# Moving the loads of a seven-product kernel's last step: rows into T, late rows into two other buffers, a recombination put first

## The chip, the cores and the metric

The kernel runs on one core of a Trainium2 chip. The core has TensorE (PE; its weight loads are listed as PEld), VectorE (DVE), ScalarE (ACT), GpSimd (POOL) and SyncE (SP). SP's work here is to issue DMAs. GpSimd and ScalarE issue some too. The metric is the time of one execution on the device in microseconds. Three executions of the kernel before gave 893.77, 895.12 and 897.36 us, so the median is 895.12. The profiled execution took 893.32 us.

## The reference: what is computed

One layer on a sequence of 512 tokens (a grid of 8 by 64) with 2048 channels, all in float32:

```python
h = RMSNorm_pre(x)
q, k, v, z = split(h @ na_w_in, 4)         # each 512 x 2048, 16 heads of 128
o = neighbourhood_attention(q, k, v, rpb)  # window of 8 x 16 tokens, bias rpb, softmax
y = (o * silu(z)) @ na_w_out               # 512 x 2048
x = x + RMSNorm_post(y)
```

The input projection is 512 x 2048 by 2048 x 8192, the output projection 512 x 2048 by 2048 x 2048.

## The kernel before, in words

**Steps.** Both projections are cut into steps. Steps 0 to 7 make q, k, v and z of two heads each. Steps 8 and 9 make the two halves of the output projection. Steps 0 and 8 are plain: two column blocks (n=0 and 1) times sixteen slices of the contraction. The other steps multiply 2x2 blocks with seven products in place of eight (Strassen's scheme in Winograd's form). Each of these has seven passes of eight slices. A pass accumulates into a chain X, Y or Z of two PSUM banks (u7Z is chain Z of step 7), and after it `combine` adds the chains into the results. In the last step (LAST, step 9) the passes run in the order `LATE = (6, 0, 1, 3, 4, 5, 2)`.

**Rows.** The work is numbered by m, from 0 to N-1 = 511. A row m is one 128x512 tile of weights that takes part in the products of slice m. The plain step 8 is m=424 to 455, the last step m=456 to 511: P6 is 456 to 463, P0 464 to 471, P1 472 to 479, P3 480 to 487, P4 488 to 495, P5 496 to 503. Pass P2, 504 to 511, is prepared early as "late rows", between the rows of other passes, because nothing follows it that would hide its preparation. `prep(m)` makes a row ready: for some passes VectorE first adds a freshly loaded tile to the running sum T[k] (`t0` to `t7`); then ScalarE writes the high part `hi` (fp32r) and VectorE the low part `lo`, the source minus the high part. TensorE multiplies hi, hi and lo. hi and lo live in rings of three buffers. Rows are prepared AHEAD = 2 ahead of use. Late rows have their parts written into the tiles `a{k}_1` and `a{k}_3` of the activations (A), whose old contents are no longer used.

**Loads.** `load_raw` loads fresh tiles into a ring of four buffers ("raw"). Each load waits until VectorE has let go of the tile four before it, in the order in which VectorE releases them. `load_t` loads straight into T[k]. One sum of the last step (T1 in the change's name) is prepared during the plain step: eight tiles `zw0` to `zw7` are loaded into two buffers (`load_z`), VectorE adds `raw512` to `raw519` to them (`sum_prep`), and the eight sums are stored to DRAM (`wsum`, `keep_z`) and fetched back into T later. The residual x is loaded by `load_res` into tiles `xres` (for token blocks t=1, 2, 3) and into T[0..3] (t=0). The gated attention outputs go to DRAM (`graw`) and are fetched back on GpSimd's queue (`fetch_g`, tile gr12 among them); all the other loads go out on SP's queue.

**Attention beside it.** `HEAD` lists the operations of each head with a delay in units of m. At the end of head 15, the transposed probabilities (pt15_0, pt15_1) are split into high and low parts, TensorE multiplies them by v into o15, and `gated` writes zm15 from o15. o15 lies in the ring of PSUM banks that the accumulators j=2, 3 of the plain step's second column block use as well.

**What sets the order.** Calls through `sync`, `dve` and `act` are kept in program order on their engine. Everything else is placed by a scheduler that starts from the program order of the loop at the end (`prep`, then the products, then whatever `beside` lists for m). Each engine then runs its list strictly in order, so an instruction that waits holds up all behind it.

**The end.** `finish` weighs one block of the result: ScalarE squares it and sums, VectorE multiplies by the post norm's gain. For the last block (i=3) VectorE works out the mean square (`msy`), GpSimd raises it to the power -0.5, and `final` scales, adds the residual and sends the rows out.

Of the kernel before, what the change touches and what calls it, by code (L numbers as in the profile page):

```python
# [28 lines left out]
WARM = 8  # L29
# [39 lines left out]
def na_block(ctx: ExitStack, tc: tile.TileContext, xT, x, gpre, gpost, w, rpb, out):  # L69
# [61 lines left out]
    def load_z(k):  # L131
        Z[k] = cp.tile([P, L], F32, tag="zw", name=f"zw{k}", bufs=2)
        nc.sync.dma_start(Z[k], w[LAST, B12, k])

    def keep_z(k):
        nc.sync.dma_start(wsum[k], Z.pop(k))
# [87 lines left out]
    def is_raw(m):  # L224
        step, p, _ = where(m)
        return step in PLAIN or p not in ((0, 1, 6) if step == LAST else (0, 6))

    def late_prep(m):

        i, rest = divmod(m - (N - 4 * KH + 1), 3)  # L230
        return [N - KH + i] if 0 <= i < KH and not rest else []

    def sum_prep(m):

        m -= base(NSTEP)
        at_m = {6 + 2 * k: [k] for k in range(KH)}
        for k in range(KH):
            at_m.setdefault(22 + 2 * k if k < KH - 2 else 15 + 2 * k, []).append(KH + k)
        return [N + j for j in at_m.get(m, ())]
# [4 lines left out]
    seq = [m for m in preps if m >= N or is_raw(m)]  # L244
# [5 lines left out]
    def load_raw(m):  # L250
        raws[m] = wp.tile([P, L], F32, tag="raw", name=f"raw{m}", bufs=NRAW)
        if m >= N:
            i, k = divmod(m - N, KH)
            nc.sync.dma_start(raws[m], w[LAST, (B11, B22)[i], k])
            return
        step, p, k = where(m)
        if step in PLAIN:
            src = w[step, (B11, B12, B21, B22)[p + 2 * (k // KH)], k % KH]
        else:
            src = w[step, (None, B12, B21, B22, B21, B22, B22)[p], k]  # L260
        (sync if m < 3 else nc.sync).dma_start(raws[m], src)
# [3 lines left out]
    def prep(m):  # L265
# [22 lines left out]
        nc.vector.tensor_tensor(lo, src, hi.bitcast(F32), ALU.subtract)  # L288
        if plain:
            if step == 0 and p == 1 and k >= KH:  # L290
                load_t(1, B11, k - KH)
        elif p == 4 and step < LAST:
            load_t(step, B12, k)
        elif p == 5 and step < LAST:
            nc.vector.tensor_tensor(T[k], T[k], src, ALU.add)  # L295
        elif p == 6 and (step + 1 < NSTEP or step == LAST and k < KH - 2):
            load_t(min(step + 1, LAST), B11, k)
        elif p == 0 and step == LAST:
            nc.sync.dma_start(T[k], wsum[k])
# [12 lines left out]
    def mm_plain(m):  # L312
# [14 lines left out]
        if k == KT - 1:  # L327
            ops.sort(key=lambda op: op[2])
        for l, r, j, i in ops:
# [56 lines left out]
    def combine(step, p):  # L386
# [29 lines left out]
        else:  # L416
            for s in range(2):
                nc.vector.tensor_tensor(c["21"][:, s, :], u[s], c["21"][:, s, :], ALU.subtract)
                nc.vector.tensor_tensor(c["22"][:, s, :], c["22"][:, s, :], u[s], ALU.subtract)  # L419
# [289 lines left out]
    def finish(n, t, src, dst=None):  # L709
# [7 lines left out]
        def weigh():  # L717
            nc.scalar.activation(rest, src, AF.Square, accum_out=part[:, t, i : i + 1])
            nc.vector.tensor_tensor(y, src, gb[n], ALU.mult)  # L719
# [9 lines left out]
        if i == 3:  # L729
            nc.vector.tensor_scalar(msy[:, col], part[:, t, 3:4], 1.0 / D, ms3[:, col], ALU.mult, ALU.add)  # L730
            nc.gpsimd.tensor_tensor(rcy[:, col], msy[:, col], mhalf[:, 0:1], ALU.pow)

# [18 lines left out]
    for k in range(KH):  # L751
        at(base(NSTEP) + 1 + 2 * k, load_z, k)
# [6 lines left out]
    for q in range(4):  # L759
        at(base(LAST) + 4 + 3 * q, load_res, 1, q)  # L760
        at(base(LAST) + 4 * KH + 3 + 2 * q, load_res, 0, q)
    for i in range(KH):
        at(base(LAST) + 2 * KH + 5 * i // 2, load_res, 2 + i // 4, i % 4)
# [12 lines left out]
    for m in range(-AHEAD, N):  # L776
        if m + AHEAD < N - KH:
# [7 lines left out]
        (mm_plain if where(m)[0] in PLAIN else mm_seven)(m)  # L785
# [57 lines left out]
```

## Time and profile before

| | |
|---|---|
| median of three executions | 895.12 us (893.77 to 897.36) |
| profiled execution | 893.32 us, of which 891.5 us from the first to the last instruction (span) |
| granted TensorE clock | 0.998 of full speed |
| TensorE busy | 876.9 us, 98% of the span |
| VectorE, ScalarE, GpSimd busy | 734.3, 559.4 and 20.9 us |
| DMA | 174.95 MB, 196 GB/s on average |

The busy line says how long each engine worked. The lists of waits say for which group of instructions an engine stood idle and how long in total, how many times, and the longest. In a timeline each row has its start in microseconds, its length, the engine, the line, the operation and its tiles (numbers left out), and in brackets how long the engine was idle before it and what released it. `x4` means four instructions in a row. A table of windows has, for each stretch, its length, the busy time and the instructions of each engine, the granted clock, the busy share of the DMA engines and GB/s.

### The profile page before, as it was taken

How to read it: one execution, taken by the hardware profiler on the slowest of the kernel's cores; microseconds unless marked ns; L12 is line 12 of the kernel's file. 1: busy time of each engine (PE TensorE's matmuls, PEld its weight loads, DVE VectorE, ACT ScalarE, POOL GpSimd, SP SyncE). 2: the span in 40 equal slices, each digit the busy share in tenths (PEclk: the TensorE clock that was granted, in tenths of full speed). 3: DMA queues.
4: the chain of work that ended last, by engine and by line, in shares of the span. 5: the costliest groups of instructions: out<-in, count | busy, mean ns of one | idle time of the engine just before them, and what ended most of it. 6: DMA issues, size and time to landing. Idle time of an engine off the chain costs nothing. (4 is left out here: it accounts for less than half of the span.)

```text
span 891.5 us, 13143 instructions
## 1 busy us (share of the span) xinstructions
PE 876.9 (98%) x4176; PEld 729.5 (82%) x4176; DVE 734.3 (82%) x1370; ACT 559.4 (63%) x1091; POOL 20.9 (2%) x42
## 2 busy tenths in 40 slices
PE   9999999999999999999999999999999999999995
PEld 8888888888888888888888888888888787888874
DVE  5467979897988898889879987998799855896995
ACT  7566857585758575856675667566756755446551
POOL 0000000000000000000000000000010100000000
PEclk9999999999999999999999999999999999999999
DMA  8768357635663676376547653764487566677875
GB/s 274 228 182 255 98 172 234 204 126 181 238 190 112 215 217 188 106 232 217 168 124 234 209 175 119 243 208 154 137 267 224 169 225 213 204 234 228 254 223 170
DMA packets 91734, 174.95 MB, mean 196 GB/s; under 512 B 10512, under 2 KB 10512, under 8 KB 91664
## 3 DMA queue, kind: packets, MB, share of 16 engines
q1 hardware_dynamic: 88992, 166.24, 60.1%
q0 software_dynamic: 2240, 7.34, 2.4%
q8 instruction: 32, 0.52, 0.2%
q10 hardware_dynamic: 432, 0.53, 0.2%
q14 instruction: 38, 0.31, 0.1%
HBM read 164.11 MB, written 9.96 MB: 195 GB/s over the span
## 5 line engine op out<-in xcount | busy, mean ns | idle before, releaser
L287 ACT CAST hi<-t 128x512 fp32r<-128x512 f32 x318 | 196.0, 619 | 127.7 <-DVE lo L288 29.2
L288 DVE TENSOR_TENSOR lo<-t,hi 128x512 fp32r<-128x512 f32 x318 | 217.0, 689 | 38.3 <-ACT hi L287 36.5
L288 DVE TENSOR_TENSOR lo<-raw,hi 128x512 fp32r<-128x512 f32 x184 | 126.1, 689 | 53.3 <-ACT hi L287 40.1
L287 ACT CAST hi<-raw 128x512 fp32r<-128x512 f32 x180 | 111.5, 620 | 90.9 <-DMA raw<-in_w 21.7
L330 PE MATMUL u<-hi,a 128*128 128x512 f32 x512 | 131.7, 394 | 1.2 <-DVE e L419 1.1
L277 DVE TENSOR_TENSOR t<-t,raw 128x512 f32<-128x512 f32 x184 | 123.1, 688 | 3.5 <-DMA raw<-in_w 3.0
L330 PEld LDWEIGHTS u<-hi,a 128*128 128x128 f32 x512 | 95.5, 189 | 21.5 <-DVE e L419 1.7
L330 PE MATMUL u<-lo,a 128*128 128x512 f32 x256 | 70.8, 390 | 0.0
L330 PEld LDWEIGHTS u<-lo,a 128*128 128x128 f32 x256 | 48.1, 188 | 10.1
L295 DVE TENSOR_TENSOR t<-t,raw 128x512 f32<-128x512 f32 x56 | 37.3, 688 | 7.3 <-DMA raw<-in_w 7.3
L377 PE MATMUL u9Y<-hi,a 128*128 128x512 f32 x96 | 26.8, 394 | 1.4 <-ACT hi L287 1.3
L377 PE MATMUL u5Y<-hi,a 128*128 128x512 f32 x96 | 26.9, 397 | 0.0
L377 PE MATMUL u3Y<-hi,a 128*128 128x512 f32 x96 | 26.9, 397 | 0.0
L377 PE MATMUL u4Y<-hi,a 128*128 128x512 f32 x96 | 26.9, 397 | 0.0
L377 PE MATMUL u6Y<-hi,a 128*128 128x512 f32 x96 | 26.9, 397 | 0.0
L377 PE MATMUL u7Y<-hi,a 128*128 128x512 f32 x96 | 26.8, 396 | 0.0
L377 PE MATMUL u1Y<-hi,a 128*128 128x512 f32 x96 | 26.8, 396 | 0.0
L377 PE MATMUL u2Y<-hi,a 128*128 128x512 f32 x96 | 26.8, 396 | 0.0
L377 PEld LDWEIGHTS u9Y<-hi,a 128*128 128x128 f32 x96 | 17.7, 188 | 6.3 <-ACT hi L287 2.3
L608 POOL DMA_DIRECT2D graw<-zm x14 | 7.8, 555 | 561.4 <-DVE zm L602 561.4
L558 ACT ACTIVATE edge<-edge,col 128x192 f32<-128x192 f32 x32 | 14.5, 454 | 8.9 <-DVE col L551 8.9
L377 PEld LDWEIGHTS u4Y<-hi,a 128*128 128x128 f32 x96 | 17.4, 189 | 3.2
(447 smaller groups left out, 1935.0 us busy)
## 6 DMA issues: line engine op xcount, KB each, us to landing
raw<-in_w SPq DMA_DIRECT2D x392, 256.0 KB, 3.0
t<-in_w SPq DMA_DIRECT2D x126, 256.0 KB, 2.9
bm<-in_rpb SPq DMA_DIRECT2D x16, 384.0 KB, 4.5
x<-in_xT SPq DMA_DIRECT2D x16, 256.0 KB, 3.8
graw<-zm POOLq DMA_DIRECT2D x14, 256.0 KB, 3.5
sq<-in_x SPq DMA_DIRECT2D x6, 512.0 KB, 5.3
xres<-in_x SPq DMA_DIRECT2D x12, 256.0 KB, 4.1
zw<-in_w SPq DMA_DIRECT2D x10, 256.0 KB, 2.7
```

Source lines behind the costliest of these rows:

```text
L277: nc.vector.tensor_tensor(T[k], T[k], src, ALU.add)
L287: (act if m < 4 else nc.scalar).copy(hi, src)
L288: nc.vector.tensor_tensor(lo, src, hi.bitcast(F32), ALU.subtract)
L295: nc.vector.tensor_tensor(T[k], T[k], src, ALU.add)
L330: nc.tensor.matmul(U[n][j], l, r, start=k == 0 and i == 0, stop=k == KT - 1 and i == 2)
L377: nc.tensor.matmul(U[c][s], l, r, start=begins(step, p) and k == 0 and n == 0, stop=k == KH - 1 and n == 2, skip_group_check=True,)
L558: nc.scalar.activation(p, p, AF.Exp, bias=nm[:, i : i + 1], accum_out=sm[:, i : i + 1])
L608: nc.gpsimd.dma_start(graw[h], z_of[h])
```

## The change

Six things change.

1. Eight warming matmuls at the start become nine (`WARM`).
2. `load_z` and `keep_z` go out from GpSimd's queue in place of SP's. From k=2 the loads stand 2 m later; the eight additions (`sum_prep`) come one m later. The first two loads have nothing to wait for and stand at the start of GpSimd's list.
3. In the last step the rows of pass P5 are loaded into T by `load_t`, each after pass P4's row has left T, and no longer through the ring.
4. The late rows 504 to 511 use the two "zw" buffers, which are free by then, and are prepared 4 m earlier, from m = N-35, every third m.
5. At the last m of step 7 the products and the recombination are written before the next `prep`; the recombination's four operations and the next low part are kept in order on VectorE. The plain step's first products are sorted so that those of accumulators j=0 and 1 come first.
6. The residual loads stand at other m. In `finish`, the last block of t=0 and 1 works out `msy` before the multiplication by the gain.

```diff
-WARM = 8
+WARM = 9
...
     def load_z(k):
         Z[k] = cp.tile([P, L], F32, tag="zw", name=f"zw{k}", bufs=2)
-        nc.sync.dma_start(Z[k], w[LAST, B12, k])
+        nc.gpsimd.dma_start(Z[k], w[LAST, B12, k])
     def keep_z(k):
-        nc.sync.dma_start(wsum[k], Z.pop(k))
+        nc.gpsimd.dma_start(wsum[k], Z.pop(k))
...
-        return step in PLAIN or p not in ((0, 1, 6) if step == LAST else (0, 6))
+        return step in PLAIN or (p in (3, 4, 2) if step == LAST else p not in (0, 6))
     def late_prep(m):
-        i, rest = divmod(m - (N - 4 * KH + 1), 3)
+        i, rest = divmod(m - (N - 5 * KH + 5), 3)
...
-        at_m = {6 + 2 * k: [k] for k in range(KH)}
+        at_m = {7 + 2 * k: [k] for k in range(KH)}
...
-    seq = [m for m in preps if m >= N or is_raw(m)]
+    seq = [m for m in preps if m >= N or is_raw(m) and m < N - KH]
+    for m in range(N - KH, N):
+        at_prep.setdefault(m - 2 if m > N - KH + 1 else N - 6 * KH, []).append(m)
...
     def load_raw(m):
-        raws[m] = wp.tile([P, L], F32, tag="raw", name=f"raw{m}", bufs=NRAW)
+        if N - KH <= m < N:
+            raws[m] = cp.tile([P, L], F32, tag="zw", name=f"raw{m}", bufs=2)
+        else:
+            raws[m] = wp.tile([P, L], F32, tag="raw", name=f"raw{m}", bufs=NRAW)
...
-        nc.vector.tensor_tensor(lo, src, hi.bitcast(F32), ALU.subtract)
+        (dve if m == base(NSTEP) + 1 else nc.vector).tensor_tensor(lo, src, hi.bitcast(F32), ALU.subtract)
...
-        elif p == 4 and step < LAST:
-            load_t(step, B12, k)
+        elif p == 4:
+            load_t(step, B22 if step == LAST else B12, k)
...
         if k == KT - 1:
             ops.sort(key=lambda op: op[2])
+        elif step and n == 0 and k == 0:
+            ops.sort(key=lambda op: max(op[2], 1))
...
+            vector = dve if step + 1 == NSTEP else nc.vector
             for s in range(2):
-                nc.vector.tensor_tensor(c["21"][:, s, :], u[s], c["21"][:, s, :], ALU.subtract)
-                nc.vector.tensor_tensor(c["22"][:, s, :], c["22"][:, s, :], u[s], ALU.subtract)
+                vector.tensor_tensor(c["21"][:, s, :], u[s], c["21"][:, s, :], ALU.subtract)
+                vector.tensor_tensor(c["22"][:, s, :], c["22"][:, s, :], u[s], ALU.subtract)
...
-            nc.vector.tensor_tensor(y, src, gb[n], ALU.mult)
+            if i < 3 or t > 1:
+                nc.vector.tensor_tensor(y, src, gb[n], ALU.mult)
...
-            nc.vector.tensor_scalar(msy[:, col], part[:, t, 3:4], 1.0 / D, ms3[:, col], ALU.mult, ALU.add)
+            (dve if t < 2 else nc.vector).tensor_scalar(msy[:, col], part[:, t, 3:4], 1.0 / D, ms3[:, col], ALU.mult, ALU.add)
             nc.gpsimd.tensor_tensor(rcy[:, col], msy[:, col], mhalf[:, 0:1], ALU.pow)
+            if t < 2:
+                dve.tensor_tensor(y, src, gb[n], ALU.mult)
...
-        at(base(NSTEP) + 1 + 2 * k, load_z, k)
+        at(base(NSTEP) + (3 if k > 1 else 1) + 2 * k, load_z, k)
...
-        at(base(LAST) + 4 * KH + 3 + 2 * q, load_res, 0, q)
+        at(base(LAST) + 5 * KH + q, load_res, 0, q)
...
-        at(base(LAST) + 2 * KH + 5 * i // 2, load_res, 2 + i // 4, i % 4)
+        at(base(LAST) + 2 * KH + 1 + 2 * i, load_res, 2 + i // 4, i % 4)
...
     for m in range(-AHEAD, N):
+        if m == base(NSTEP) - 1:
+            mm_seven(m)
         if m + AHEAD < N - KH:
             prep(m + AHEAD)
...
-        (mm_plain if where(m)[0] in PLAIN else mm_seven)(m)
+        if m != base(NSTEP) - 1:
+            (mm_plain if where(m)[0] in PLAIN else mm_seven)(m)
```

Three places of the instruction lists, in which the numbers behind a name only count tiles. The first is VectorE at the boundary from step 7 to the plain step (lo425 to lo427 are low parts of the plain step's rows, a5_0 to a6_1 low parts of activations, s5 and e the recombination that reads u7Z). Before:

```order
L160 TENSOR_TENSOR a4_1_121<-t4_140,a4_1_121 128x256
L160 TENSOR_TENSOR a5_0_124<-t5_141,a5_0_124 128x256
L288 TENSOR_TENSOR lo425_7443<-raw425_7362,hi425_7442 128x512
L418 TENSOR_TENSOR s5_7_6785<-u7Z0_7094,s5_7_6785 128x512
L419 TENSOR_TENSOR e_7_7070<-e_7_7070,u7Z0_7094 128x512
L418 TENSOR_TENSOR s5_7_6785<-u7Z1_7095,s5_7_6785 128x512
L419 TENSOR_TENSOR e_7_7070<-e_7_7070,u7Z1_7095 128x512
L288 TENSOR_TENSOR lo426_7463<-raw426_7375,hi426_7462 128x512
```

Now:

```order
L161 TENSOR_TENSOR a4_1_122<-t4_141,a4_1_122 128x256
L161 TENSOR_TENSOR a5_0_125<-t5_142,a5_0_125 128x256
L161 TENSOR_TENSOR a5_1_126<-t5_142,a5_1_126 128x256
L65 TENSOR_TENSOR s5_7_6786<-u7Z0_7095,s5_7_6786 128x512
L65 TENSOR_TENSOR e_7_7071<-e_7_7071,u7Z0_7095 128x512
L65 TENSOR_TENSOR s5_7_6786<-u7Z1_7096,s5_7_6786 128x512
L65 TENSOR_TENSOR e_7_7071<-e_7_7071,u7Z1_7096 128x512
L65 TENSOR_TENSOR lo425_7458<-raw425_7363,hi425_7457 128x512
```

lo425 moved behind the recombination, and a5_1 ahead of it.

The second is VectorE around o15 in the plain step. Before:

```order
L288 TENSOR_TENSOR lo438_7929<-raw438_7831,hi438_7928 128x512
L269 TENSOR_TENSOR zw5_7924<-zw5_7924,raw517_7932 128x512
L288 TENSOR_TENSOR lo439_7960<-raw439_7873,hi439_7959 128x512
L486 TENSOR_TENSOR pt15_0l_7955<-pt15_0_7949,pt15_0h_7954 128x512
L288 TENSOR_TENSOR lo440_7992<-raw440_7900,hi440_7991 128x512
L269 TENSOR_TENSOR zw6_7987<-zw6_7987,raw518_7995 128x512
L486 TENSOR_TENSOR pt15_1l_7983<-pt15_1_7977,pt15_1h_7982 128x512
L288 TENSOR_TENSOR lo441_8030<-raw441_7935,hi441_8029 128x512
L602 SCALAR_TENSOR_TENSOR zm15_7812<-o15_8012,zm15_7812 128x512
```

Now:

```order
L296 TENSOR_TENSOR lo438_7928<-raw438_7830,hi438_7927 128x512
L296 TENSOR_TENSOR lo439_7956<-raw439_7869,hi439_7955 128x512
L498 TENSOR_TENSOR pt15_0l_7951<-pt15_0_7945,pt15_0h_7950 128x512
L276 TENSOR_TENSOR zw5_7986<-zw5_7986,raw517_7959 128x512
L296 TENSOR_TENSOR lo440_7991<-raw440_7899,hi440_7990 128x512
L498 TENSOR_TENSOR pt15_1l_7982<-pt15_1_7976,pt15_1h_7981 128x512
L296 TENSOR_TENSOR lo441_8026<-raw441_7931,hi441_8025 128x512
L276 TENSOR_TENSOR zw6_8063<-zw6_8063,raw518_8029 128x512
L614 SCALAR_TENSOR_TENSOR zm15_7808<-o15_8008,zm15_7808 128x512
```

The additions into zw5 and zw6 stand later; that into zw6 is now behind pt15_1l and directly ahead of zm15.

The third is in the last step: ScalarE around P1's last rows (hi476 to hi480 are rows of passes P1 and P3, a0_1 to a3_1 the high parts of the late rows 504 to 507). Before:

```order
L287 CAST a0_1_105<-raw504_8689 128x512
L287 CAST hi476_8685<-t4_140 128x512
L287 CAST hi477_8699<-t5_141 128x512
L287 CAST hi478_8711<-t6_142 128x512
L287 CAST a1_1_109<-raw505_8755 128x512
L287 CAST hi479_8721<-t7_143 128x512
L287 CAST hi480_8734<-t0_136 128x512
L287 CAST hi481_8747<-t1_137 128x512
```

Now:

```order
L294 CAST a0_1_106<-raw504_8536 128x512
L294 CAST hi476_8688<-t4_141 128x512
L294 CAST a1_1_110<-raw505_8538 128x512
L294 CAST hi477_8698<-t5_142 128x512
L294 CAST hi478_8718<-t6_143 128x512
L294 CAST a2_1_114<-raw506_8706 128x512
L294 CAST hi479_8730<-t7_144 128x512
L294 CAST a3_1_118<-raw507_8751 128x512
```

Late rows now come every third cast, a2_1 ahead of hi479 and a3_1 ahead of hi480. On SP's list in the same step the loads `t0<-in_w` to `t7<-in_w` (pass P5) stand in place of raw496 to raw503, and the four residual loads into T come directly behind them.

## The prediction, made before the changed kernel was run

> **What bounds the kernel now.** I read the page's busy line first, then TensorE's waits, then the stages of the end.
>
> ```profile
> span 891.5 us, 13143 instructions
> PE 876.9 (98%) x4176; PEld 729.5 (82%) x4176; DVE 734.3 (82%) x1370; ACT 559.4 (63%) x1091; POOL 20.9 (2%) x42
> ...
> PE u9Y L377 <- ACT hi L287: 1.3, 1, 1.3
> PE o L596 <- DVE pt_1l L486: 1.1, 1, 1.1
> PE u L330 <- DVE e L419: 1.1, 1, 1.1
> ```
>
> TensorE is busy for 876.9 of 891.5 us, and the change removes no matmul. So 14.6 us is all there is to win, and only what TensorE waits for counts. Three waits of over 1 us lie inside the program. The rest is the start and the tail after the last matmul. Each edit is therefore priced by the wait that it touches.
>
> **Recombination first** (boundary of step 7 and the plain step).
>
> ```profile
> 702.04 0.76 DVE L160 TENSOR_TENSOR a<-t,a 128x256 fp32r<-128x256 f32 x2
> 702.71 0.69 DVE L288 TENSOR_TENSOR lo<-raw,hi 128x512 fp32r<-128x512 f32 x1
> 703.31 0.69 DVE L418 TENSOR_TENSOR s<-u7Z,s 128x512 f32<-128x512 f32 x1
> 703.91 0.68 DVE L419 TENSOR_TENSOR e<-e,u7Z 128x512 f32<-128x512 f32 x1
> ...
> 704.64 0.74 PE L330 MATMUL u<-hi,a 128*128 128x512 f32 x2 [1.07 <-DVE e L419]
> ```
>
> TensorE's new accumulators j=2,3 reuse u7Z's banks and wait until VectorE has read them. The change takes one low part (lo425) from ahead of the four recombination operations: 703.31-702.71 = 0.60. But the order shows one small subtraction (a5_1) put in front of them, half of the pair of 0.76, so 0.34 by pitch. What is left is **-0.2** (0 to -0.3). Sorting j=0,1 first moves no matmul across the boundary, and j=2 still waits for the first e.
>
> **The wait before o15.** Here VectorE's order decides.
>
> ```profile
> 750.46 3.50 DMA raw<-in_w
> ...
> 750.65 0.69 DVE L288 TENSOR_TENSOR lo<-raw,hi 128x512 fp32r<-128x512 f32 x1
> 754.04 0.69 DVE L269 TENSOR_TENSOR zw<-zw,raw 128x512 f32<-128x512 f32 x1 [2.69 <-DMA raw<-in_w]
> 754.65 0.68 DVE L486 TENSOR_TENSOR pt_1l<-pt,pt_1h 128x512 fp32r<-128x512 f32 x1
> ...
> 756.65 0.69 DVE L602 SCALAR_TENSOR_TENSOR zm<-o,zm 128x512 f32<-128x512 f32 x1 [0.72 <-PE o L596]
> ...
> 755.39 0.39 PE L596 MATMUL o<-pt_1l,vh 128*128 128x256 f32 x1 [1.15 <-DVE pt_1l L486]
> ...
> DMA to landing us min/median/max: 3.0/3.4/5.0
> ```
>
> The addition into zw6 (754.04) waited 2.69 us for raw518, issued at 750.46. Behind it stood pt15_1l, and TensorE idled 1.15. Now pt15_1l and lo441 stand ahead of that addition, so these 1.15 us go. The next instruction that can be late is zm15: it stands right behind the addition, and accumulator u8_1_3 takes o15's bank, so TensorE waits for it. With the stall gone o15 ends 1.15 us earlier and zm15 could start at 756.65-1.15 = 755.50. The ring gives raw518 its buffer after row 440's low part, which ended at 751.34 and may now end up to 0.6 sooner: I take 751.05. With the landings of this window (the last row) it arrives at 754.05, 754.5 or 756.05. The addition is over 0.65 later, at 754.7, 755.15 or 756.7: zm15 is in time in the first two cases and 1.2 late in the third, which hands the whole gain back. So -1.15 to +0.05; a landing of 5.6, worse than any here, would make it +0.6. I take **-0.8**, near the median's end.
>
> **P3's rows and the late rows** (last step). The raw ring feeds the end late:
>
> ```profile
> SPq L261 <- DVE a L288: 6.8, 3, 6.4
> ...
> 850.00:854.00 4.00, 4.00 (x19) 3.30 (x19) 4.00 (x9) 1.09 (x2) 0.00 (x0) 1.00 0.02 7
> 854.00:862.00 8.00, 8.00 (x36) 6.35 (x35) 7.54 (x16) 5.22 (x12) 0.14 (x1) 1.00 0.87 265
> ...
> 866.93 1.07 PE L377 MATMUL u9Y<-hi,a 128*128 128x512 f32 x4
> 868.10 0.73 PE L377 MATMUL u9Y<-lo,a 128*128 128x512 f32 x2
> 868.66 0.62 PE L377 MATMUL u9X<-a,a 128*128 128x512 f32 x2
> 870.55 0.96 PE L377 MATMUL u9Y<-hi,a 128*128 128x512 f32 x3 [1.26 <-ACT hi L287]
> ...
> 869.88 0.62 ACT L287 CAST hi<-raw 128x512 fp32r<-128x512 f32 x1 [2.29 <-DMA raw<-in_w]
> ```
>
> SP's queue stood 6.4 us behind one release; DMA then fell to a share of 0.02 and afterwards ran at 0.87, with rows and residual together. TensorE paid for it near 868. A matmul costs 0.23 by pitch, so four from 866.93 should end at 867.84, two from 868.10 at 868.56, two from 868.66 at 869.11; the followers came 0.26, 0.10 and 1.44 later, 1.8 in all. After the change these eight rows go straight into T, each buffer free after the matching low part of the pass before, eight rows ahead of use (six matmuls each at 0.23, 11 us), and the residual no longer stands between them. That cover exceeds the 3.5 us median and the 5.1 maximum of a row's landing: **-1.8**; at worst, where they share the DMA engines with the residual, two thirds of the stall stays (-0.6).
>
> Two things go against it. ScalarE's strict order now has a2_1<-raw506 ahead of hi479:
>
> ```profile
> 827.45 0.69 DVE L288 TENSOR_TENSOR a<-raw,a 128x512 fp32r<-128x512 f32 x1
> ...
> 830.96 0.62 ACT L287 CAST a<-raw 128x512 fp32r<-128x512 f32 x1 [0.48 <-DMA raw<-in_w]
> 831.48 0.62 ACT L287 CAST hi<-t 128x512 fp32r<-128x512 f32 x1
> ...
> 834.19 0.62 PE L377 MATMUL u9Y<-hi,a 128*128 128x512 f32 x2
> ...
> DMA to landing us min/median/max: 2.6/3.5/5.1
> ```
>
> raw506 follows raw504 into its buffer, freed at 827.45+0.69 = 828.14. It lands at 830.8, 831.7 or 833.3, where nothing is lost until about 831. At the median hi479 starts at 832.3 instead of 831.48 and is ready at 832.9, still 1.3 ahead of its matmul (834.19). At the maximum it is ready at 834.5 and its low part, needed 0.45 after it, about 1.0 late; with the next cast behind it I put the bound at +1.3, and take **+0.2**. The second lies in pass P4, where VectorE is 4.00 of 4.00 busy (850 to 854 above): a5_3's low part and row 494's addition into T now stand ahead of lo493, which was ahead of both. Two operations are 1.2 by pitch; two matmuls of u9X moved up there (0.46) fill part of it: **+0.1** (0 to +0.7).
>
> **The head.** zw0 and zw1 now go out from GpSimd's queue at about 1.5 us, where they went from SP's at 32, and there is a ninth warming matmul.
>
> ```profile
> 4.00:8.00 4.00, 3.91 (x14) 3.10 (x14) 3.56 (x8) 3.48 (x8) 0.00 (x0) 1.00 1.03 356
> ...
> 1.05 3.78 PE L97 MATMUL warm<-ones 128*128 128x128 f32 x16 [1.05 <-DVE ones L94]
> 4.92 2.83 PE L330 MATMUL u<-hi,a 128*128 128x512 f32 x8
> ...
> 7.08 0.69 DVE L288 TENSOR_TENSOR lo<-raw,hi 128x512 fp32r<-128x512 f32 x1
> ```
>
> DMA is full there, so two more transfers of 256 KB push the rest back by up to 524/356 = 1.5 us. The second row's low part (7.08 to 7.77) is wanted at about 9.4, so 1.6 us of cover stands against it. The warm matmuls are 16 records in 3.87 us, 0.24 each; the ninth adds two, of which part sits in the wait for the first row. **+0.2** (0 to +0.7).
>
> **The tail.**
>
> ```profile
> 883.03 0.69 DVE L719 TENSOR_TENSOR c<-u9X,gpost 128x512 f32<-128x512 f32 x1 [1.23 <-ACT ysq L718]
> 883.63 0.20 DVE L730 TENSOR_SCALAR rows<-part,rows 128x1 f32<-128x1 f32 x1
> 884.50 1.41 DVE L737 SCALAR_TENSOR_TENSOR xres<-y,rows,xres 128x512 f32<-128x512 f32 x2 [0.66 <-POOL rows L731]
> 883.92 0.54 POOL L731 TENSOR_TENSOR rows<-rows,mhalf 128x1 f32<-128x1 f32 x1 [4.90 <-DVE rows L730]
> ```
>
> The two operations change places: the small one starts at 883.03, GpSimd's power 0.60 earlier (883.32 to 883.86), and the multiply runs beside it (883.23 to 883.9). The last outputs follow: **-0.6** (-0.4 to -0.6).
>
> **GpSimd's queue.** 18 DMAs of zw and its sums leave SP. SP is idle between issues, so that alone is worth 0; what it could cost is the first rival. gr12's fetch now stands behind the store of zw3, but that addition comes ahead of zm14, before the 735.04 at which the fetch went out.
>
> **Sum.** -0.2 -0.8 -1.8 +0.2 +0.1 +0.2 -0.6 = **-2.9** on the profiled run of 893.32: 890.4. Ends: -0.3-1.15-1.8-0.6 = -3.85, and 0+0.6-0.6+1.3+0.7+0.7-0.4 = +2.3. The median shown, 895.12, lies 1.8 above the profiled run, so I forecast a median of **892.1**.
>
> **Rivals.** (a) GpSimd's transfers come late, and it ends slower. Every addition into zw stands in VectorE's order, and each buffer goes through add, store and load before its next add.
>
> ```profile
> DMA to landing us min/median/max: 2.5/3.0/6.4
> ...
> DMA to landing us min/median/max: 2.6/3.4/5.9
> ```
>
> The first row is zw on SP's queue, the second graw on GpSimd's. Adds came 754.04-748.84 = 5.2 apart, so a buffer has 10.4. It needs 0.7+3.4+3.4 = 7.5 at GpSimd's median: 2.9 to spare. At 5.9 for both it needs 12.5, 2.1 too many for each of three reuses: 6.3 less the 2.7 that VectorE idles there, +3.6, and with the other gains alone (-2.9 without o15's 0.8 is -2.1) 894.8 profiled, 896.6 as a median. It decides from 4.9 us per transfer. The Trainium skill ("SBUF — State Buffer", "SBUF: two separate sides") says that GpSimd cannot write a DMA's descriptors while an operation of VectorE holds the port that the two share, so that the DMA looks blocked. By that rule (a) is the likely case; the trace does not bear it out, since graw's median is 0.4 above zw's beside a VectorE 82% busy.
>
> (b) The in-order waits on raw518 and raw506 eat the gain: -2.9+0.8+0.05-0.2+1.3 = -0.9, 892.4 profiled, 894.2. For it: landings of 5.0 and 5.1 occur in both windows. Against: the medians fit.
>
> (c) All covers hold and the start is free: -3.85, 889.5 profiled; with the profile's small waits it may reach -4.5, 890.6 as a median.
>
> (d) The transfers were hidden or the rows merely wait elsewhere (T's loads share DMA with four residual loads right behind them): P3's term is -0.6, total -1.7, 893.4.
>
> **How the numbers follow.** Forecast (-2 to -3.7) 0.48, (a) 0.07, (b) 0.15, (c) 0.17, (d) 0.13. About 0.5%, 4.5 us, is what this measurement can tell from no change. The forecast is -0.33%, so most of it falls within; faster gets (c) and a few hundredths of the forecast, 0.20; slower by over 0.5% gets the worse part of (a) and mishaps, 0.06; within, 0.74. The range runs from (c)'s median less the 1.2 us by which the median may come closer to the profile, 889.4, to (b) and the lower part of (a), 895.8.
>
> **What would show it.** Right: no wait of o on pt_1l; no wait of u9Y on hi near 868 and no 6 us block of SP's queue; the last power 0.6 us earlier against the last matmul; u on e shorter by 0.2. Wrong: a wait of u on zm (b), of hi479 or s5 behind a<-raw (b), zw adds waiting for zw's own load (a), a first row after 5.4 us. A span gain over 4.5 or under 1 us would mean that a term here is mis-sized.

## The result, and the profile after

The changed kernel took 900.09 us (median of 7, 898.25 to 902.9) against 895.12. The ratio is 1.0054, with a 95% interval of 1.0035 to 1.0072. It is slower, by 5 us, where a gain of 3 was forecast, and it lies 4 us above the range. The profiled execution took 898.97 us, 5.65 more than that of before.

The page's first lines and the largest of TensorE's waits, of the changed kernel:

```profile
span 897.2 us, 13164 instructions
PE 880.4 (98%) x4178; PEld 731.4 (82%) x4178; DVE 733.5 (82%) x1370; ACT 560.3 (62%) x1091; POOL 31.7 (4%) x60
...
PE u L341 <- DVE zm L614: 3.3, 1, 3.3
PE u9Y L388 <- DVE s L451: 1.1, 1, 1.1
PE warm L97 <- DVE ones L94: 1.1, 1, 1.1
PE u L341 <- DVE e L65: 0.8, 1, 0.8
...
PE tz L485 <- DVE k14l L498: 0.3, 1, 0.3
```

Two of the three waits of over 1 us are gone (o on pt_1l, u9Y on hi near the end). Two new ones stand there: u on zm, and u9Y on s. And TensorE is busy 3.5 us longer than before, for the same matmuls but the one for warming. To see where the time goes, the table takes the first matmul of some rows m in both traces and gives how far the changed kernel is behind the kernel before there, in us:

```
row m            2    229   425   434   441   478   481   497   503   last matmul   end of span
behind by      0.5    0.2   1.7   2.8   7.3   7.3   8.3   8.8   6.3       6.1           5.7
```

The large step is between rows 434 and 441, at o15. VectorE there, and the chain of waits:

```profile
753.39 0.69 DVE L276 TENSOR_TENSOR zw<-zw,raw 128x512 f32<-128x512 f32 x1 [1.47 <-DMA raw<-in_w]
754.00 0.68 DVE L296 TENSOR_TENSOR lo<-raw,hi 128x512 fp32r<-128x512 f32 x1
754.60 0.68 DVE L498 TENSOR_TENSOR pt_1l<-pt,pt_1h 128x512 fp32r<-128x512 f32 x1
...
760.89 0.69 DVE L276 TENSOR_TENSOR zw<-zw,raw 128x512 f32<-128x512 f32 x1 [3.54 <-DMA raw<-in_w]
761.50 0.68 DVE L614 SCALAR_TENSOR_TENSOR zm<-o,zm 128x512 f32<-128x512 f32 x1
...
755.00 5.76 DMA raw<-in_w
```

pt15_1l (754.60) no longer waits. But the addition into zw6 (760.89) waits 3.54 us for raw518, and zm15 (761.50) stands behind it. raw518 went out at 755.00 and landed 5.76 us later. TensorE waits for zm15, and then it is slow:

```profile
757.83 1.09 PE L341 MATMUL u<-hi,a 128*128 128x512 f32 x4
762.23 3.36 PE L341 MATMUL u<-hi,a 128*128 128x512 f32 x7 [3.31 <-DVE zm L614]
...
758.00:760.00 2.00, 0.93 (x4) 0.40 (x3) 0.00 (x0) 0.00 (x0) 0.00 (x0) 1.00 0.93 363
760.00:762.00 2.00, 0.00 (x0) 0.00 (x0) 1.11 (x2) 0.00 (x0) 0.67 (x2) 0.71 0.40 105
762.00:764.00 2.00, 1.77 (x4) 1.48 (x5) 0.87 (x2) 0.62 (x1) 0.42 (x1) 0.50 0.79 209
...
766.00:768.00 2.00, 2.00 (x7) 1.57 (x6) 1.06 (x2) 1.62 (x5) 0.28 (x1) 0.58 0.45 125
768.00:770.00 2.00, 2.00 (x10) 1.64 (x10) 1.80 (x4) 1.96 (x6) 0.00 (x0) 1.00 0.05 14
```

In the rows of windows the last three numbers are the granted clock, the busy share of the DMA engines and GB/s. The clock falls to 0.50 while TensorE idles and stays there until about 767.5. Matmuls start 0.43 us apart in that time instead of 0.23, so some twelve of them cost 2.4 us on top of the wait of 3.3. That is most of the 3.5 us of "busy" time that was added. 5.7 less the 1.2 won at pt15_1l is the step of 4.5 in the table.

Of the 2.6 us that are lost between rows 229 and 434, 1.7 come before row 423 and 0.9 after row 426, with the recombination between them. Up to row 423 (steps 1 to 7) the instruction lists are the same, and the fifteen profiles used below (all but that of e11, which ran at a granted clock of 0.75) are 0.0 to 3.3 us behind the kernel before between rows 229 and 423 as well: the profiled run of the kernel before had a good draw there. From row 426 on it is the later additions. The first of them, into zw0, now stands directly ahead of k14l, a low part of head 14 that TensorE waits for:

```profile
715.05 0.69 DVE L276 TENSOR_TENSOR zw<-zw,raw 128x512 f32<-128x512 f32 x1 [0.56 <-DMA raw<-in_w]
715.66 0.68 DVE L498 TENSOR_TENSOR k14l<-tk,k14h 128x512 fp32r<-128x512 f32 x1
...
716.40 0.44 PE L485 MATMUL tz<-ident,s 128*128 128x128 f32 x2 [0.32 <-DVE k14l L498]
```

The eight profiles in which this addition comes one row later (this one, e1, e2, e8, e9, e13, e14 and e15) lose 0.5 to 1.5 us between rows 426 and 428. The others lose nothing there.

The second new wait, where pass P3 begins; ScalarE, then TensorE:

```profile
839.52 0.62 ACT L294 CAST a<-raw 128x512 fp32r<-128x512 f32 x1 [1.72 <-DMA raw<-in_w]
840.04 0.62 ACT L294 CAST hi<-t 128x512 fp32r<-128x512 f32 x1
...
844.62 0.70 PE L388 MATMUL u9Y<-hi,a 128*128 128x512 f32 x2 [1.14 <-DVE s L451]
...
875.47 1.07 PE L388 MATMUL u9Y<-hi,a 128*128 128x512 f32 x4
876.37 0.62 PE L388 MATMUL u9Y<-lo,a 128*128 128x512 f32 x2
```

a2_1 (839.52) waits for raw506, hi479 behind it is late, VectorE's work piles up behind that, and s5 releases TensorE 1.14 us late. The last two rows are from the end of pass P5: no idle time is left there, and the table falls from 8.8 to 6.3. The tail:

```profile
889.14 0.21 DVE L65 TENSOR_SCALAR rows<-part,rows 128x1 f32<-128x1 f32 x1 [1.84 <-ACT ysq L730]
889.43 0.54 POOL L744 TENSOR_TENSOR rows<-rows,mhalf 128x1 f32<-128x1 f32 x1 [4.90 <-DVE rows L65]
890.01 1.42 DVE L753 SCALAR_TENSOR_TENSOR xres<-y,rows,xres 128x512 f32<-128x512 f32 x2
```

### The profile page after: what moved, and what is told of

It is laid out like the page before. It is cut to its first block, busy times and chain, and to the rows that moved or that the text cites. A ratio compares the mean times of both kernels' runs of the same rounds, so it can differ in the third digit from the quotient of the medians.

```text
span 897.2 us, 13164 instructions
## 1 busy us (share of the span) xinstructions
PE 880.4 (98%) x4178; PEld 731.4 (82%) x4178; DVE 733.5 (82%) x1370; ACT 560.3 (62%) x1091; POOL 31.7 (4%) x60
## 4 chain that ended last, share of the span: by engine, by line
PE 84%; DMA 6%; DVE 5%; issue 3%; ACT 1%; POOL 0%; SPq 0%; DVEq 0%; POOLq 0%; ACTq 0%
PE u L341 17%; DMA raw<-in_w 5%; PE u2Y L388 4%; PE u4Y L388 4%; PE u3Y L388 4%; PE u1Y L388 4%; PE u9Y L388 3%; PE u5Y L388 3%; PE s L537 3%; PE u9Z L388 2%; PE u3X L388 2%; PE u2X L388 2%; PE u4X L388 2%; PE u6Z L388 2%; PE u5Z L388 2%
## 5 line engine op out<-in xcount | busy, mean ns | idle before, releaser
L294 ACT CAST hi<-t 128x512 fp32r<-128x512 f32 x326 | 200.6, 619 | 130.5 <-DVE lo L296 30.1
L296 DVE TENSOR_TENSOR lo<-t,hi 128x512 fp32r<-128x512 f32 x326 | 221.5, 686 | 38.8 <-ACT hi L294 37.8
L296 DVE TENSOR_TENSOR lo<-raw,hi 128x512 fp32r<-128x512 f32 x175 | 119.5, 687 | 53.4 <-ACT hi L294 38.9
L294 ACT CAST hi<-raw 128x512 fp32r<-128x512 f32 x172 | 106.4, 621 | 87.2 <-PE u L341 21.7
L341 PE MATMUL u<-hi,a 128*128 128x512 f32 x512 | 134.2, 398 | 4.3 <-DVE zm L614 3.3
L161 DVE TENSOR_TENSOR a<-x,a 128x256 fp32r<-128x256 f32 (+1 forms) x22 | 10.5, 519 | 11.9 <-ACT a L160 10.6
L388 PEld LDWEIGHTS u3Y<-hi,a 128*128 128x128 f32 x96 | 17.4, 188 | 3.2
```

What stands on the lines that cost most here:

```text
L161: (vector or nc.vector).tensor_tensor(lo, src, hi.bitcast(F32), ALU.subtract)
L294: (act if m < 4 else nc.scalar).copy(hi, src)
L296: (dve if m == base(NSTEP) + 1 else nc.vector).tensor_tensor(lo, src, hi.bitcast(F32), ALU.subtract)
L341: nc.tensor.matmul(U[n][j], l, r, start=k == 0 and i == 0, stop=k == KT - 1 and i == 2)
L388: nc.tensor.matmul(U[c][s], l, r, start=begins(step, p) and k == 0 and n == 0, stop=k == KH - 1 and n == 2, skip_group_check=True,)
```

## The experiments

Sixteen kernels ran, each against the kernel before on the same chip. Theory S says that the order did it: zm15 behind an addition whose row lands late. Theory Q says that GpSimd's queue made the loads late. Theories L, G, A and others came up on the way. Each heading gives the median and the ratio to the kernel before with its interval; the experiments ran on several chips, so kernels are compared by the ratios. Waits and landing times come from one profiled execution of each kernel.

**e1: nothing ahead of zm15.** 896.75 us, 1.0017 (1.0004 to 1.0029).

```diff
-        at_m = {7 + 2 * k: [k] for k in range(KH)}
+        at_m = {7 + 2 * k + 2 * (k == 6): [k] for k in range(KH)}
```

> The changed kernel with one of its eight additions moved: that of raw518 into zw6 comes two rows later, so that zm15 no longer stands behind it on VectorE. Theory S (the order: zm15 behind an addition whose row lands late; a stall of 3.3 us and then about 2.4 us of half clock): the wait of u on zm goes, 5.7 us come back, about 894.4 us (893.5 to 895.5). Theory Q (the transfers on GpSimd's queue make all loads land later, the order only shows it): the loss appears at another wait, 899 or more. Theory C (the loss lies in the other parts or in chance): 899 to 900.

The entries of k=6 and k=7 fall on one row, and the second replaces the first. So the kernel that ran leaves out the addition of raw518 into zw6 and its load altogether. The wait of u on zm went and the clock was full there. Not 5.7 but 3.3 us came back. Its profile has a new stall of 1.9 us at the program's second row (below, e14 to e16).

**e2: the zw transfers back on SP.** 899.0 us, 1.0050 (1.0031 to 1.0069).

```diff
-        nc.gpsimd.dma_start(Z[k], w[LAST, B12, k])
+        nc.sync.dma_start(Z[k], w[LAST, B12, k])
-        nc.gpsimd.dma_start(wsum[k], Z.pop(k))
+        nc.sync.dma_start(wsum[k], Z.pop(k))
```

> The changed kernel with the zw loads and the stores of the sums back on SP's queue; the later additions and their order on VectorE stay. S: zm15 still stands behind the addition into zw6 and raw518 is issued at about the same moment, so a wait of u on zm of 1 to 4 us stays: 896 to 900. Q: raw518 lands in 3 to 3.5 us, no wait of u on zm, 894 or less.

The wait stays, on whichever queue; from the waits and VectorE's timeline:

```profile
PE u L341 <- DVE zm L614: 3.8, 1, 3.8
...
760.92 0.69 DVE L276 TENSOR_TENSOR zw<-zw,raw 128x512 f32<-128x512 f32 x1 [4.00 <-DMA raw<-in_w]
761.53 0.68 DVE L614 SCALAR_TENSOR_TENSOR zm<-o,zm 128x512 f32<-128x512 f32 x1
```

S holds: the later additions alone put zm15 behind a load. And the load is late here too, with all the zw transfers on SP. It went out at 755.61, 5.3 us before the addition that waits for it began:

```profile
753.39 0.33 SPq L134 DMA_DIRECT2D zw<-in_w  x1
753.81 1.23 SPq L268 DMA_DIRECT2D raw<-in_w  x2
755.09 0.42 SPq L65 DMA_DIRECT2D gpost<-in_gpost  x1
755.61 0.38 SPq L261 DMA_DIRECT2D raw<-in_w  x1
```

The zw load had waited for the store of a sum, and what stood behind it then went out together: raw518 is the fifth transfer in 2.2 us. So a crowd around raw518 does not need GpSimd's queue.

**e3: the additions at their old place, GpSimd's queue kept.** 898.16 us, 1.0037 (1.0023 to 1.0052).

```diff
-        at_m = {7 + 2 * k: [k] for k in range(KH)}
+        at_m = {6 + 2 * k: [k] for k in range(KH)}
```

> The changed kernel with the eight additions at their old place (one row earlier), the zw transfers still on GpSimd's queue. S: no wait of u on zm, the old wait of o on pt_1l of about 1.1 us is back, full clock throughout: about 895.5. Q: rows land 1.5 us later than before here too, the wait of o on pt_1l is 2.5 us or more: 897 to 899.

No wait of u on zm; the old wait of o on pt_1l is back at 2.1 us where the kernel before had 1.1, with half clock behind it. The time is Q's, and the wait lies between what S and Q expected. The queue, or the loads' times and the two early loads that stay with it, does damage of its own.

**e4: all about zw as before.** 894.59 us, 0.9998 (0.9985 to 1.0011). The edits of e2 and e3, and:

```diff
-        at(base(NSTEP) + (3 if k > 1 else 1) + 2 * k, load_z, k)
+        at(base(NSTEP) + 1 + 2 * k, load_z, k)
```

> The changed kernel with everything about zw as before (queue, load times, additions); what is left is the last step's rows, the recombination, the tail and the ninth warming matmul. S and Q both: the old wait of o on pt_1l of 1.1 us, and the gains of the rest: last step's rows -1.8, tail -0.4, recombination -0.2, head +0.3, which makes -2.1, about 893 against 895.1. C: 896 or more.

By the ratios 5.0 us come back, so the zw part makes the whole loss. But the rest wins nothing clear of the interval, where 2.1 were expected. Against the kernel before this kernel is 0.5 us behind at row 478, 2.9 at row 481, 3.4 at row 497 and 0.9 at row 503: it loses 2.4 us where P3 begins and wins 2.5 at the end. ScalarE and TensorE where it loses:

```profile
834.13 0.62 ACT L294 CAST a<-raw 128x512 fp32r<-128x512 f32 x1 [3.14 <-DMA raw<-in_w]
834.66 0.61 ACT L294 CAST hi<-t 128x512 fp32r<-128x512 f32 x1
...
839.23 0.69 PE L388 MATMUL u9Y<-hi,a 128*128 128x512 f32 x2 [1.43 <-DVE s L451]
```

raw506 was issued at 828.67, when its buffer was free, and its cast began at 834.13; hi479 stood behind it.

**e5: late rows in the ring again.** 891.88 us, 0.9970 (0.9957 to 0.9982). e4 with eight warming matmuls, and:

```diff
-    seq = [m for m in preps if m >= N or is_raw(m) and m < N - KH]
+    seq = [m for m in preps if m >= N or is_raw(m)]
-    for m in range(N - KH, N):
-        at_prep.setdefault(m - 2 if m > N - KH + 1 else N - 6 * KH, []).append(m)
...
-            raws[m] = cp.tile([P, L], F32, tag="zw", name=f"raw{m}", bufs=2)
+            raws[m] = wp.tile([P, L], F32, tag="raw", name=f"raw{m}", bufs=NRAW)
...
-        i, rest = divmod(m - (N - 5 * KH + 5), 3)
+        i, rest = divmod(m - (N - 4 * KH + 1), 3)
```

> Everything about zw and the number of warming matmuls as before; the rows of pass P5 go into T as in the change, but the late rows 504 to 511 are back in the ring of four buffers and at their old places. In e4 TensorE lost 2.5 us where pass P3 begins, behind the high part of late row 506, and won 2.4 at the end. Theory L (the late rows' two buffers lose what P5's rows in T win): the wait of u9Y on s of 1.4 us goes, the gain at the end stays, about 892.3 us. Theory E (T's rows or the residual loads fill the DMA engines and so delay whatever is loaded there): the loss of about 2.5 us stays at the start of P3, 894.5.

L holds on the time, 2.5 us under e4 by the ratios, and the end keeps its gain (from 1.9 behind at row 497 to 0.7 ahead at 503). The wait of u9Y on s does not go, it is 1.3 in this profile; what goes is the delay of hi479 ahead of it. The loss from row 478 to 481 is 1.1 in place of 2.4.

**e6: and zw6 behind zm15.** 890.79 us, 0.9958 (0.9939 to 0.9976).

```diff
-        at_m = {6 + 2 * k: [k] for k in range(KH)}
+        at_m = {6 + 2 * k + 3 * (k == 6): [k] for k in range(KH)}
-        at(base(NSTEP) + 5 + 2 * k, keep_z, k)
+        at(base(NSTEP) + 5 + 2 * k + 2 * (k == 6), keep_z, k)
```

> As e5, and the addition of raw518 into zw6 comes three rows later, behind zm15, with its store two rows later, so that neither pt15_1l nor zm15 stands behind it. Theory L and theory S together: the wait of o on pt_1l (0.8 in e4) goes as well, about 891.3 us, 0.4% under the kernel before. If the order around o15 does not matter, it is equal to e5.

Neither pt_1l nor zm is among TensorE's waits any more. The largest:

```profile
PE warm L97 <- DVE ones L94: 1.1, 1, 1.1
PE u L336 <- DVE e L65: 0.9, 1, 0.9
PE u9Y L383 <- DVE s L446: 0.7, 1, 0.7
```

This version beats both kernels: by the ratios 3.8 us under the one before and 8.6 under the changed one.

**e7: the queue alone.** The kernel before with e2's edit the other way round; with nothing to wait for, the first two zw loads go to the program's start. 897.74 us, 1.0034 (1.0018 to 1.0050).

> The kernel before, with the zw loads and the stores of the sums on GpSimd's queue and nothing else. S alone (the queue is harmless, the order does the damage): 895 to 896. Q (transfers on GpSimd's queue land later): e3 over e4, which differ by the queue and the loads' times, was +3.6, of which 1.3 at the wait of o on pt_1l: 897.5 to 898.6, with that wait at 2 us or more and, by the two early loads, a stall of up to 1 us at the second row.

Q's figure. VectorE and SP at o15:

```profile
757.87 0.69 DVE L271 TENSOR_TENSOR zw<-zw,raw 128x512 f32<-128x512 f32 x1 [3.79 <-DMA raw<-in_w]
...
750.12 0.33 SPq L263 DMA_DIRECT2D raw<-in_w  x1
750.50 0.43 SPq L65 DMA_DIRECT2D gpost<-in_gpost  x1
751.02 0.38 SPq L263 DMA_DIRECT2D raw<-in_w  x1
751.46 0.42 SPq L65 DMA_DIRECT2D gpost<-in_gpost  x1
751.97 0.38 SPq L256 DMA_DIRECT2D raw<-in_w  x1
```

raw518 goes out at 751.97 as the fifth transfer in 1.9 us on SP alone. In the kernel before, raw518 went out ahead of a zw load for which SP waited until 753.03, and a row and a gpost load came behind that wait; raw518 landed after 3.5 us. Here the addition begins 5.9 us after the issue. At o15 (rows 434 to 441) this costs 1.1 us in the profile; at the second row, which waits 1.7 us, it is 1.2 behind.

**e8: the zw part alone on the kernel before.** 900.26 us, 1.0063 (1.0043 to 1.0083). (The kernel before with the change's edits to `load_z`, `keep_z`, their places and `at_m`.)

> The kernel before, with the whole change to zw (queue, load times, additions one row later) and nothing else. S: a wait of u on zm of 2 to 4 us with half clock behind it; the parts add up: the changed kernel over e4 was +5.5, so about 900.5. If the loss needs the other parts: under 898.

As S had it to 0.3 us; the wait of u on zm is 2.6 us here, with half clock behind it.

**e9: three gpost loads later.** 895.91 us, 1.0015 (1.0003 to 1.0027).

```diff
-        at(base(NSTEP) + 11 + n, load_gb, n)
+        at(base(NSTEP) + (11 if n == 0 else 21) + n, load_gb, n)
```

> The changed kernel with three of the four loads of the post norm's gain (gpost, 256 KB each) moved some ten rows later, past the end of o15. In the changed kernel SP issued raw441, raw442, two gpost loads and raw518 and GpSimd a store of a sum within a few microseconds, and raw518 landed 5.8 us after its issue. Theory G (with the zw transfers off SP nothing spaces its queue, the transfers bunch, and raw518 shares the DMA engines with gpost): raw518 lands in at most 4 us, the wait of u on zm falls from 3.3 to about 1 us, no half clock behind it, 895 to 897. Theory H (GpSimd's transfers are what delays it): raw518 lands after 5 us or more, 899 to 900.

```profile
757.91 0.69 DVE L276 TENSOR_TENSOR zw<-zw,raw 128x512 f32<-128x512 f32 x1 [1.00 <-DMA raw<-in_w]
758.51 0.68 DVE L614 SCALAR_TENSOR_TENSOR zm<-o,zm 128x512 f32<-128x512 f32 x1
...
754.32 0.33 SPq L261 DMA_DIRECT2D raw<-in_w  x1
...
PE u L341 <- DVE zm L614: 0.8, 1, 0.8
```

raw518 takes 3.5 us again; it went out at 754.32, and the addition began at 757.91. The wait falls to 0.8, and the clock stays full. Theory G holds in its main part: the order made zm15 depend on this load, and the gpost loads beside it made the load late. Its other part, that the zw transfers have to leave SP for this, does not: e2 had the crowd with them on SP.

**e10: e7 with gpost later.** 894.64 us, 1.0007 (0.9997 to 1.0017).

> As e7 (only the queue of the zw transfers changed), with the same three gpost loads later. G: raw518 lands in at most 4 us, where it took 5.8 in e7, and the wait of o on pt_1l falls from 2.2 to 1.2 us or less: about 896.5. H: it stays at 2 us, 897.5 or more. The rest of e7's loss (the head) stays in both.

```profile
PE o L600 <- DVE pt_1l L490: 0.2, 1, 0.2
```

G again, by more than expected: 2.4 of e7's 3.0 us come back (by the two ratios), and the wait of o on pt_1l is below that of the kernel before. So part of the 2.4 may be what later gpost loads would win in any case; the kernel before with this edit alone was not run.

**e11: both orders changed back, on GpSimd's queue.** 895.03 us, 1.0004 (0.9995 to 1.0014). e5's edit and e1's on the changed kernel, with e1's table: it too leaves out the addition of raw518 and its load.

> The changed kernel with both orders mended and the zw transfers still on GpSimd's queue: the addition into zw6 and its store two rows later, behind zm15, and the late rows back in the ring of four at their old places. If the losses add up: e1 was 3.4 under the changed kernel, e5 2.7 under e4, so 894.0 us; against e6 (890.8, the same on SP's queue with the old times) that leaves 3.2 for GpSimd's queue, as e7 had over the kernel before. If the queue costs nothing once the orders are mended: 891.

A miss of 1.0 us by the medians and 1.5 by the ratio.

**e12: e6 with gpost later.** 891.07 us, 0.9962 (0.9949 to 0.9975).

> As e6 (zw on SP's queue with the old times but for zw6, the late rows in the ring), with the three gpost loads later. G: a little less bunching, 890 to 890.8; if SP's waits for the sums already space the queue enough, equal to e6, 890.8. Either way under the kernel before by 0.4% or more.

Equal to e6, but this is no test of G. In both kernels the addition into zw6 stands behind zm15, so TensorE no longer waits for what stands behind raw518. The load itself is quicker: from its issue to the addition 2.8 us pass here and 4.0 in e6.

**e13: the complete addition behind zm15.** 896.27 us, 1.0016 (1.0003 to 1.0029).

```diff
-        at_m = {7 + 2 * k: [k] for k in range(KH)}
+        at_m = {7 + 2 * k + 3 * (k == 6): [k] for k in range(KH)}
-        at(base(NSTEP) + 5 + 2 * k, keep_z, k)
+        at(base(NSTEP) + 5 + 2 * k + 3 * (k == 6), keep_z, k)
```

> The changed kernel with the addition of raw518 into zw6, complete, three rows later, behind zm15, and its store behind it. In e1 and e11 two entries of the table fell on one row and the addition and its load were left out, so that they showed zm15 with nothing ahead of it and 256 KB less to load. Theory S: what mattered there was that zm15 did not wait; 896.5 to 897, as e1. If the missing load made e1 faster: 898 or more.

Equal to e1, so what e1 left out did not matter: moving one addition by three rows is worth 3.4 us (from 1.0054 to 1.0016).

**e14: both orders and gpost mended, zw on GpSimd's queue.** e13's, e5's and e9's edits. 894.86 us, 1.0003 (0.9992 to 1.0015).

> As e13, with the late rows back in the ring at their old places and three gpost loads later; the zw transfers stay on GpSimd's queue, zw0 and zw1 at the start. If the queue itself costs little (e10 over the kernel before: +0.6), the losses are the two orders and the bunching and nothing else: 891 to 892. If the queue costs as much as in e7 (+3.2): 894 or more.

A miss: 3 us above what was expected. In its profile it is 0.7 us behind the kernel before at the second row and 3.7 at row 425, before any of the mended places.

**e15: e14 with the first two zw loads on SP, eight warming matmuls.** 893.98 us, 0.9975 (0.9962 to 0.9987).

```diff
-        nc.gpsimd.dma_start(Z[k], w[LAST, B12, k])
+        (nc.sync if k < 2 else nc.gpsimd).dma_start(Z[k], w[LAST, B12, k])
```

> As e14, but zw0 and zw1 are loaded on SP's queue at their old place (at 32 us, not at the start), with eight warming matmuls. e14 missed its number (894.9 where 891 to 892 was expected) and its profile was 3.7 us behind the kernel before already at the plain step. Theory A (the two early loads cost it, in the first rows and after): 891.5 to 892.5. Theory B (GpSimd's queue, or the later additions, cost it around the plain step): 894 or more.

**e16: e12 with only these two loads on GpSimd's queue at the start.** 893.39 us, 0.9979 (0.9966 to 0.9992).

> As e12 (891.1; everything on SP's queue), but zw0 and zw1 go out from GpSimd's queue at the start. A: the two loads alone cost what e14 lost, 893.5 to 895, with a wait of u on hi of about 1 us at the second row. B: 891 to 891.8.

```profile
PE u L336 <- ACT hi L65: 1.6, 1, 1.6
```

By the ratios the two early loads cost 2.5 us between e14 and e15, which differ by a warming matmul as well, and 1.5 between e12 and e16, where the intervals overlap; so theory A has most of it. What is left between e15 and e12 is 1.2 us for the queue and the later additions, within the intervals. e15's profile shows a place for it: TensorE waits 1.2 us for k14l behind the addition into zw0, and e12, with that addition at its old place, does not. The first part of A's cost is at the second row. In the ten profiles with the early loads TensorE waited there 0.2, 1.9, 1.1, 1.7, 0, 0.6, 1.3, 0.6, 1.1 and 1.6 us (after, e1, e3, e7, e8, e9, e10, e13, e14, e16), mean 1.0; in those without them 0 to 0.5. Part of e14's 3.7 us comes later, in steps 1 to 7, where the lists of instructions are those of the kernel before. Some profiles with the early loads have such delays (e8, e13, e14) and some don't (e10, e16). Two without these loads have them too, against the kernel before: e2 and e4 lose 1.5 and 1.3 us between rows 229 and 423. What makes them stays open.

## Why the prediction was wrong, point by point

**The wait before o15 (forecast -0.8, measured +4.5).** This is the step that failed. The place was right, and so was the mechanism: pt15_1l's stall went, and zm15 behind raw518 is rival (b). (b) priced it at +0.05 and missed as well, with 894.2. Three things in the price were wrong. The landing was bounded by 3.0 to 5.0 us from a window of the kernel before, with other transfers beside the load; the change alters which transfers go out with it, and it took 5.76. The queue alone brings that (e7, 5.77 us), and so do the later loads and additions with everything on SP (e2, 5.3 us to the addition). With three gpost loads out of the way it took 3.5 (e9). The issue came later too: the addition into zw5 waited 1.47 us for raw517, so row 440's low part ended at 754.68, and raw518 went out at 755.00. That is 1.2 later than 751.05 shifted by the 2.8 us that the kernel was behind there. And a price for the clock was missing: the sum counted a wait as its own length, and behind a wait of 3.3 us came 2.4 us of half clock. The bound "+0.6" could not hold that. With the addition behind zm15 3.4 us come back (e13), with the gpost loads later 3.5 (e9).

**The additions at row 427 and at zm14 (no term).** The prediction priced the later additions at o15 alone. The one into zw0 also stands directly ahead of k14l, the one into zw3 ahead of zm14; in the changed kernel 0.9 us are lost there, between rows 426 and 434.

**GpSimd's queue (forecast 0).** "SP is idle between issues, so that alone is worth 0" was wrong. e7 shows +3.0 us for it alone, of which e10 takes back 2.4 by moving gpost. SP's idle time was not free: its waits on the stores of the sums decided which loads went out together. The 3.0 include the two early loads, which the prediction priced at the head and which e10 keeps. Rival (a), which had the queue's transfers themselves late, is not what happened: its deciding point was 4.9 us per transfer, and in the plain step of the changed kernel the zw loads took 3.4 and the stores 3.8 us in the median, on SP 2.7 and 3.2; and around o15 the additions waited for raw517 and raw518, not for zw's own loads. The Trainium skill ("DMA: Bandwidth & Descriptors", "Issuing engines are not separate DMA queues") says that DMAs issued by several engines run on the same 16 DMA engines and interleave, and that a second issuer saves only the time of issuing. No run here speaks against it. e7 and e10 add that what a queue waits for can matter more than the time of issuing.

**P5's rows in T (under "P3's rows" in the prediction; forecast -1.8, measured -2.6).** Right in mechanism, and a little better in size: 2.6 us are won from row 497 to 503 in all thirteen profiles with the edit, 0.4 at most in e7, e8 and e10, which lack it. The late rows beside it were mis-sized. "+0.2" at the start of P3 measured 1.0 in the changed kernel and 2.4 in e4 (rows 478 to 481): raw506's cast began 5.5 us after its issue in e4 (828.67 to 834.13), over the maximum of 5.1 that bounded it, and the bound of 1.3 left out the queue behind hi479 on VectorE. Even e5, with the late rows as before, loses 1.1 there against the profiled run of the kernel before, so that run had a good draw at this place. The nine profiles with the late rows in the ring lose 0.5 to 1.7 there, mean 1.1, and the seven with the two buffers 1.0 to 4.7, mean 2.4; so the two buffers cost about 1.3, and the 1.0 of the changed kernel is a good draw as well. Together with the recombination, the tail and the ninth warming matmul the two edits are worth about nothing (e4); with the late rows left in the ring, P5's rows in T, the recombination and the tail together are worth 2.7 us (e5 against the kernel before).

**The head (forecast +0.2, 0 to 0.7).** In the profile of the changed kernel it came out as forecast: a wait of 0.2 us, 0.5 behind at the second row. Over all profiles it is mis-sized: a wait of 1.0 us at the second row in the mean, 1.9 at most, and 1.5 to 2.5 us in the time (e16, e15). The cover of 1.6 us was set against a mean delay of 1.5 on a full DMA, and taken as enough.

**Recombination (forecast -0.2).** The wait of u on e is 0.8 in the changed kernel and 0.6 to 0.9 in nearly all those that have the edit, against 1.1 before and 0.9 to 1.1 in e7, e8 and e10, which don't. As forecast, though too small to show in the time.

**The tail (forecast -0.6).** Right: the last group of outputs begins 1.69 us after the last matmul's end (890.01 less 888.32) in place of 2.29, and 0.46 of these 0.60 reach the end of the span.

**P4 (forecast +0.1)** measured +0.5 between rows 481 and 497 in the changed kernel, within its range of 0 to +0.7.

A slip in the sum: 890.4 and 1.8 make 892.2, not 892.1. It changes nothing.

## What to carry to other kernels

A wait that stands in a DMA queue decides which transfers go out together. Taking it away can make a crowd (e7), and so can moving what it waits for (e2). Before either, list what the queue will then send out together, and take the landing time of the load that an in-order engine waits for from that crowd and not from the old window. In an in-order list, an instruction that waits for a load belongs behind, not ahead of, the one that TensorE waits for; moving one such addition by three rows was worth 3.4 us here, three times the wait that the change removed. And a wait of TensorE should be priced with what the clock does after it.

## What the runs showed of the hardware

After an idle time TensorE can run at half clock for 3 to 5.5 us. It did after waits of 3.3 (the changed kernel), 3.8 (e2), 2.6 (e8), 2.1 (e3) and 1.9 us (e1, at the second row). It did not after 2.2 and 1.7 (e7), 1.6 (e16) and 2.7 us (e13), nor after any wait of 1.5 or less. The traces show what decides. In their records of the granted clock each stretch at one clock but the last is a whole multiple of 3.413 us: 754.35 (221 times), 6.83 (twice) and 122.88 us (36 times) in the changed kernel, 6.83, 3.41 and 873.81 us in e1. Cut into windows on this grid, e1 around its wait of 1.9 us and e13 around its wait of 2.7:

```profile
7.76:11.17 3.41, 1.50 (x7) 1.24 (x7) 1.91 (x5) 3.35 (x8) 0.00 (x0) 1.00 0.82 314
11.17:14.59 3.42, 3.42 (x10) 2.65 (x9) 2.92 (x6) 3.35 (x7) 0.00 (x0) 0.50 0.79 245
...
835.84:839.25 3.41, 1.72 (x8) 1.10 (x6) 0.00 (x0) 0.16 (x1) 0.00 (x0) 1.00 1.01 282
```

In e1 the whole wait, 1.91 us of idle time, lies in one window, and half clock begins at that window's end. In e13 the wait falls on two, with 1.69 us in the first. Half clock began at the end of the windows with 1.92 (the changed kernel), 2.11 (e2), 2.42 (e8), 2.14 (e3) and 1.91 us (e1) of idle time, and after no window of any profile with 1.85 (e7) or less. It lasted one window in e1, e3 and e8, and two in the changed kernel and e2, whose waits reached 1.4 and 1.7 us into the second. This is read from seventeen profiles; no run set out to test it.

The Trainium skill ("TensorE: Matmul & The Clock Gate", "Part 1: The HAM clock gate (the "warmup" mystery)") puts the fall to half clock at an idle window of about 3.4 us that runs freely, and gives 426.7 ns between starts of matmuls of 512 columns at half clock. The grid and the distance agree (3.413 and 0.43 us here); a window that is idle as a whole is not needed here, since 1.91 us of idle time in one were enough.
